# Turned queries in the far stretch, the last pair's sum on VectorE, and a higher rate for the last convolution, in a hybrid encoder layer

## The chip, the cores and the metric

The kernel runs on one core of one Trainium2 chip. The metric is device time in microseconds (us), the median of several executions; lower is better. The engines are TensorE (PE; its weight loads are shown as PEld), VectorE (DVE), ScalarE (ACT), GpSimd (POOL) and SyncE (SP), which issues most of the DMA transfers.

## The reference

One layer on x of 2048 tokens by 1024 channels (cut; everything is float32):

```python
y = rmsnorm(h, norm_mix_g) @ w_in                 # q, k, v (8 heads of 64), conv inputs a, g (512 each)
att = dilated_sliding_attention(q, k, v)          # three patterns, see below
conv = conformer_conv(a, g, ...)                  # a*sigmoid(g), 31 taps per channel, layernorm, silu
h = h + concat([att, conv]) @ w_out
h = h + cross_attention(rmsnorm(h), rmsnorm(mem)) # 4 heads of 256, 256 memory rows
h = h + relu(rmsnorm(h) @ w_up)**2 @ w_down
out = rmsnorm(h)

def dilated_sliding_attention(q, k, v):
    for window, d in ((128, 1), (512, 4), (2048, 16)):
        o, lse = banded_attention(to_strided(q, d), to_strided(k, d), to_strided(v, d), window // (2 * d))
        ...
    w = softmax(stack(lses), axis=0)
    return sum(w[..., None] * stack(outs), axis=0)
```

Pattern d takes every d-th token as a sequence of its own, and each query sees the keys within 64 places of it there. Here pattern 0 is d = 1, pattern 1 is d = 4, and the far pattern is d = 16. The three results of a query are added with weights that come from their log-denominators.

## The kernel before, in words

**Number format.** Every matmul operand is kept as a high and a low part (fp32r), and each product is three matmuls (`mm3`, L197 to L200): high by high, high by low, low by high. A weight tile is loaded raw, its high part is cast on ScalarE (L189), its low part is a subtraction (L190) on VectorE, or on GpSimd for the glu weights.

**Stages.** The first stages normalise x, and compute q, k, the gated convolution inputs u (`glu`) and v, in token groups of 512 (p = 0 to 3). Results go to DRAM scratch (`qscr`, `qfar`, `kscr`, `vtok`, `uscr`) and are read again in the order that each pattern needs. After them:

- *The value stage* (L737 to L747): matmuls of the second half of v. Beside them the convolution of token group 0 for channel tiles 2 and 3 (`conv0`, pinned behind VectorE's last value operation): a multiply-add on VectorE for each of 31 taps (L215), 4 to a step, and the result goes to `cscr`. `weave(steps, (conv0, 1.2))` (L746) takes 1.2 steps of it for each step of the value pipeline, and `drain(conv0)` what is left.
- *The far stretch* (L1082 to L1110): attention of token group 0 (`first = att(0, p2_)`) with the far pattern of all tokens. For each head: four far units (`att_far`), two units of pattern 1, two of pattern 0 (`order` is (1, 0), L941). A unit is: scores of query blocks into PSUM (L979; L845 and L846 for the far pattern), mask and minimum on VectorE (L762), exponential on ScalarE (L763), turns on TensorE (L769), casts (L772, L773), products with the values (L777 to L779). The units are staged so that the scores of one come ahead of the turns of another. `rest`, the remaining glu tiles and the first two output weights, fills TensorE between: 32 steps go ahead, then 0.8 steps for each of `first` (L1107, L1109). A step of `rest` is one `mm3`. `ln0` is the layernorm of group 0's convolution; it reloads `cscr` as tiles `lc` (added at L238 to L240).
- *The post stages*, p = 0 to 3: output projection with residual (`resid_linear`), cross-attention, MLP and final norm. Beside them run the attention of group p + 1, without far pattern, and its convolution. The last steps of `first` are woven with the first of post(0), and the rest of `first` is drained there: the handover.

**Queries.** `load_keys` loads a head's queries (`qh`, high twice; `ql`, low) from `qscr`. In the far stretch both heads of a pair are loaded at the pair's beginning (L1015), the heads in two slots of `qlow`, and pattern 1 takes `slice(blk, 512, 4)` of them as weights (L974): a read with a step of four floats. In the other attention stages `turned` (L806 to L811) lays them out by residue with two GpSimd copies per head, so that pattern 1 reads contiguous queries too.

**The sum of the patterns.** `combine` (L871 to L932) is one generator per pair of heads. It loads patterns 1 and 2 of the pair from DRAM (`ld` from `oscr`), computes the weights (L890 to L912; minima, exponential and reciprocal on VectorE and ScalarE, the other small ones on `W`, which is GpSimd), multiplies and adds the three results (L916, L918, on `W`), turns the sum on TensorE (L926), and splits it into a high part (ScalarE, L928) and a low part (VectorE, L929). Both go to DRAM (`cath`, `catl`). `load_cat` and `load_pair` load them again as operands of the output projection. In post(0) the last of these loads (pair j = 1 of half 1, that is k = 2 and 3) is issued late, ahead of the last two k of the first three output tiles (L1180).

**Order.** The scheduler fixes each engine's order when the program is built; engines then run their queues strictly in order, and a waiting instruction holds all behind it. SyncE's queue issues loads and stores in one order as well. `weave` and `pinned` (issue behind the last recorded instruction of the named engines) steer that order.

Of the kernel before, what the change touches and what calls it, by code (L numbers as in the profile page):

```python
# [21 lines left out]
P = 128  # L22
S = 2048
D = 1024
H = 8
# [22 lines left out]
def hybrid_layer(ctx, tc, A, out):  # L48
# [688 lines left out]
    with ExitStack() as st:  # L737
        lbv = pool("lin_v", stack=st)
        cu = pool("conv0b", stack=st)
        conv0 = pinned(conv_units(cu, 0, (2, 3), False), "dve")  # L740
        for _ in range(4):
            next(steps)
        weave(islice(steps, 8), (conv0, 1))
        for _ in range(4):
            next(steps)
        weave(steps, (conv0, 1.2))  # L746
        drain(conv0)  # L747
    early.close()

# [40 lines left out]
        dma(f(k), f(kscr[:, :, h].rearrange("x d r i -> (x d) r i")[:, :, 32 * p:32 * p + 64]))  # L790
        return k

    def load_keys(h, p, slot=0):

        k = None
        if p:
            k = keys_of(h, p)
        qh = kq.tile([P, 512], F32R, tag="qh", name=f"qh{p}{h}", bufs=2)
        ql = qlow[slot]
        cols = slice(512 * p, 512 * p + 512)  # L800
        for x in range(2):
            dma(f(qh[64 * x:64 * x + 64]), f(qscr[0, :, h, cols]))
        dma(f(ql[0:64]), f(qscr[1, :, h, cols]))
        return k, (qh, ql)
# [21 lines left out]
    def att_far(p2_, h, k, vt, q):  # L826
# [37 lines left out]
        for rq in range(4):  # L864
# [3 lines left out]
            if rq == 2 and h < H - 1:  # L868
                q[0] = far_q(h + 1, 0)

    def combine(p, pr, o0):  # L871

        if p:
            yield
        ld = aq.tile([P, 2, 4, 2, ROW], F32, tag="ld", name=f"ld{p}{pr}")
        for i in range(2):
            dma(ld[:, i].rearrange("p j h e -> p j (h e)"),
                oscr[pr][i][512 * p:512 * (p + 1)].rearrange("(j p) e -> p j e", p=P))
        yield
        yield  # L880
        if p == 0:
            for _ in range(2 if pr < 3 else 1):
                yield
        sm_ = top.tile([P, 5, 8], F32, tag="csm", name=f"csm{p}{pr}")
        e3 = top.tile([P, 3, 4, 2], F32, tag="ce", name=f"ce{p}{pr}")
        mm_ = sm_[:, 0].rearrange("p (j h) -> p j h", h=2)
        W = POOL
        with ExitStack() as st:
            after(st, "dve")
            DVE.tensor_tensor(mm_, ld[:, 0, :, :, HD + 1], ld[:, 1, :, :, HD + 1], op=ALU.min)  # L890
            DVE.tensor_tensor(mm_, mm_, o0[:, :, :, HD + 1], op=ALU.min)
        W.tensor_tensor(e3[:, 0], mm_, o0[:, :, :, HD + 1], op=ALU.subtract)
        for i in range(2):
            W.tensor_tensor(e3[:, 1 + i], mm_, ld[:, i, :, :, HD + 1], op=ALU.subtract)
        yield
        with ExitStack() as st:
            after(st, "act")
            ACT.activation(e3, e3, AF.Exp)
        d3 = sm_[:, 1:4].rearrange("p q (j h) -> p q j h", h=2)
        W.tensor_tensor(d3[:, 0], e3[:, 0], o0[:, :, :, HD], op=ALU.mult)  # L900
        for i in range(2):
            W.tensor_tensor(d3[:, 1 + i], e3[:, 1 + i], ld[:, i, :, :, HD], op=ALU.mult)
        dn = sm_[:, 4]
        W.tensor_tensor(dn, sm_[:, 1], sm_[:, 2], op=ALU.add)
        W.tensor_tensor(dn, dn, sm_[:, 3], op=ALU.add)
        yield
        with ExitStack() as st:
            after(st, "dve")
            DVE.reciprocal(dn, dn)
        d2 = dn.rearrange("p (j h) -> p j h", h=2)  # L910
        for i in range(3):
            W.tensor_tensor(e3[:, i], e3[:, i], d2, op=ALU.mult)  # L912
        at = aq.tile([P, 4, 2, HD], F32, tag="cat", name=f"cat{p}{pr}")
        for i in range(3):
            src = ld[:, i - 1, :, :, 0:HD] if i else o0[:, :, :, 0:HD]
            W.tensor_tensor(src if i else at, src, e3[:, i].unsqueeze(3).to_broadcast([P, 4, 2, HD]), op=ALU.mult)  # L916
            if i:
                W.tensor_tensor(at, at, src, op=ALU.add)  # L918
        yield
        yield  # L920
        ct = [aq.tile([P, 512], F32R, tag=f"ct{x}", name=f"ct{x}{p}{pr}") for x in "hl"]
        with ExitStack() as st:
            after(st, "pe", "act", "dve")
            pt = ps("T", f"catT{p}{pr}")
            for j in range(4):
                PE.transpose(pt[:, j * P:(j + 1) * P], at[:, j].rearrange("p h d -> p (h d)"), ident)  # L926
            vs = vinv[:, pr:pr + 1]
            ACT.activation(ct[0], pt, AF.Copy, scale=vs)  # L928
            DVE.scalar_tensor_tensor(ct[1], pt, vs, f(ct[0]), op0=ALU.mult, op1=ALU.subtract)  # L929
        for t, d in zip(ct, (cath, catl)):  # L930
            dma(f(d[pr][:, 512 * p:512 * (p + 1)]), f(t))
        yield  # L932

    def att_units(p, far, then):
# [25 lines left out]
        def unit(pr, hh, pat, g, k, q_, opt, o0):  # L960
# [6 lines left out]
            for z in range(2):  # L967
                blk = 2 * g + z
                if pat == 0:
                    qs = slice(P * blk, P * blk + P)  # L970
                    kv = k[:, :, 8 * blk + 12:8 * blk + 28].rearrange("p r (c i) -> p c r i", c=2)
                    m = 0 if 4 * p + blk == 0 else (2 if 4 * p + blk == 15 else 1)
                else:
                    qs = slice(P * blk, P * blk + P) if not far else slice(blk, 512, 4)  # L974
                    kv = k[:, blk:16:4, 0:64].rearrange("p r (c i) -> p c r i", c=2)
                    m = 3 if p == 0 else (5 if p == NG - 1 else 4)
                o = sp_[:, 256 * z:256 * z + 256]
                for x in range(2):
                    last["pe"] = PE.matmul(o, q_[x][:, qs], kv, start=x == 0, stop=x == 1)  # L979
                probs.append((pat, m, o, sm[:, 2 * z:2 * z + 2].rearrange("p c q -> p (c q)"),  # L980
                              os_[:, blk, hh, HD + 1:HD + 2]))
# [21 lines left out]
            if g and hh:  # L1003
                if pat == order[1]:
                    then(pr, o0)
                if pr < H // 2 - 1:
                    if not far:
                        load_v(pr + 1, (pat,))
                    elif not pat:
                        load_v(pr + 1, (2, 1, 0))  # L1010

        load_v(0, (2, 1, 0) if far else (0, 1))
        nxt = None if far else load_keys(0, p)
        for pr in range(H // 2):
            K = [load_keys(2 * pr + hh, p, hh) for hh in range(2)] if far else None  # L1015
            o0 = aq.tile([P, 4, 2, ROW], F32, tag="o0", name=f"o0_{p}{pr}", bufs=2)
            for hh in range(2):
                h = 2 * pr + hh
                if far:
                    k, q_ = keys, K[hh][1]  # L1020
                    if h < H - 1:
                        keys = far_keys(far, h + 1)
                    yield from att_far(far, h, k, vt, q3)
                    qs = (q_, q_)
                else:
                    k, q_ = nxt
                    qs = (q_, turned(h, p, q_))
                for pat in order:
                    opt = []
                    yield from [unit(pr, hh, pat, g, k, qs[pat], opt, o0) for g in range(2)]  # L1030
                    if not far and pat == 0 and h < H - 1:
                        nxt = load_keys(h + 1, p)

    def att(p, far=None):

# [46 lines left out]
    with ExitStack() as st:  # L1082
# [2 lines left out]
        qlow3 = low_parts(p2_, 1024, 2, "ql3")  # L1085
        p2_.tile([P, 176], F32, name="farpad")
        rest = pinned(pipeline(*(u for c in range(4) for u in glu(c, (2, 3), True)), ahead(0), ahead(1)), "pe")
        for _ in range(32):
            next(rest)

        c01 = []
# [12 lines left out]

        ln0 = pinned(conv_ln(0, ln_alloc), "pe")
        first = pinned(att(0, p2_), "pe")
        weave(islice(first, 50), (ln0, 0.33), (rest, 0.8))  # L1107
        drain(ln0)
        weave(islice(first, 74), (rest, 0.8))  # L1109
        drain(rest)  # L1110
    lin.close()

# [36 lines left out]
        rstd_col(r[:, 0:n], pc[:, 0:n], n, top)  # L1149
        return r  # L1150

    cats = {}

    def load_cat(p, half):

        d = cats.setdefault(p, {})
# [3 lines left out]
                for e in range(2):  # L1160
                    d[q, 4 * (1 - half) + 2 * j + e] = t[:, e]
        for j in range(2):
            if j == 0 or half == 0 or p:
                load_pair(p, half, j)

    def load_pair(p, half, j):
        for q, src in (("h", cath), ("l", catl)):
            for e in range(2):
                k = 4 * (1 - half) + 2 * j + e
                dma(f(cats[p][q, k]), f(src[k][:, 512 * p:512 * (p + 1)]))  # L1170

    def resid_linear(load, rhs, korder, resid, hs, ssum, key, y, name, late=None):


        for ms in ((0, 1, 2), (3,), (4,), (5,), (6,), (7,)):
            wt = [load(m) for m in ms]
            pts = {}
            for i, ks in enumerate((korder[0:4], korder[4:6], korder[6:8]) if len(ms) > 1 else (korder,)):
                if late and len(ms) > 1 and i == 2:
                    late()  # L1180
                for m, (wh, wl) in zip(ms, wt):
                    if m not in pts:
                        pts[m] = ps("mm", f"{name}{m}")
                    for k in ks:
                        mm3(pts[m], wh[:, k, :], wl[:, k, :], rhs["h", k], rhs["l", k], k == korder[0], k == korder[-1])
                    if late and ks[-1] != korder[-1]:
                        yield
                    if ks[-1] == korder[-1]:
                        h = hs[m]
# [7 lines left out]
    def post(p):  # L1197
# [9 lines left out]
        def from_x(m):  # L1207
# [5 lines left out]
        ssum = ssum_tile(f"o{p}")  # L1213
        yield from resid_linear(lambda m: wout[m] if p == 0 and m in wout else wpost(wcols(w_out, m * P), f"o{p}{m}"),
                                cats[p], [4, 5, 6, 7, 0, 1, 2, 3], from_x, hs, ssum, "x", y, f"o{p}_",
                                (lambda: load_pair(0, 1, 1)) if p == 0 else None)
        rs = rstd_from(ssum)
        DVE.tensor_scalar(rs[:, 4:8], rs[:, 0:4], -1.0, None, op0=ALU.mult)

# [192 lines left out]
```

## Time and profile before

| | us |
|---|---|
| median of 3 runs | 2933.51 |
| lowest, highest | 2924.72, 2937.39 |
| profiled execution | 2929.9 |
| its span in the trace | 2928.1 |

The span is the time from the first to the last instruction of the profiled execution; 1.8 us of that execution lie around it. The mean granted TensorE clock is 0.989 of full speed. In the profile, rows of the order in time give start, duration, engine, line, operation, tiles (out<-in), shapes and, in brackets, how long the engine had been idle and what ended that. Rows by stretch give length, then busy time and number of instructions of PE, PEld, DVE, ACT and POOL, then the granted clock, the share of the DMA engines' time in use and GB/s. Busy time of a pipelined matmul overlaps that of the next: the distance of two starts says what one costs.

### The profile page before, as it was taken

The page shows a single profiled execution, that of the slowest core. Times are in us where ns is not written, and L with a number is a line of the kernel's source. Part 1 is how long each engine was busy: PE and PEld are TensorE (multiplying, and loading weights), DVE is VectorE, ACT ScalarE, POOL GpSimd, SP SyncE. Part 2 cuts the span into 40 slices and gives each one's busy share as a digit, 9 for nine tenths or more (in the row PEclk, how much of TensorE's full clock was granted, in tenths as well). Part 3 has the DMA queues.
Part 4 walks back from the last instruction along what each step waited for, and adds up shares of the span by engine and source line. Part 5 has one row for each costly group of instructions (what it writes and reads, how often), then busy time and mean ns, then how long its engine had stood idle before and what let it go on. Part 6 is the DMA issues. An engine that isn't in the chain of part 4 may idle for free.

```text
span 2928.1 us, 42935 instructions
## 1 busy us (share of the span) xinstructions
PE 2845.6 (97%) x16396; PEld 2426.2 (83%) x16396; DVE 1845.9 (63%) x3295; ACT 1186.9 (41%) x2002; POOL 462.9 (16%) x518
## 2 busy tenths in 40 slices
PE   8999999989799999999999999999999999999999
PEld 7878789878698888888888888888888888888887
DVE  5636544555568877566697865577877555544445
ACT  5632211566435333444443344344433443432233
POOL 1335421122101220210020122000210110000000
PEclk9999999999899999999999999999999999999999
DMA  8978854799724444455344445534444355333332
GB/s 263 304 161 205 194 146 135 172 239 230 206 93 133 129 134 136 138 167 172 97 128 129 136 130 177 181 101 131 121 132 132 113 153 173 94 93 94 96 99 73
DMA packets 620806, 434.89 MB, mean 149 GB/s; under 512 B 191333, under 2 KB 549785, under 8 KB 620600
## 3 DMA queue, kind: packets, MB, share of 16 engines
q1 hardware_dynamic: 582168, 414.05, 50.3%
q10 hardware_dynamic: 38432, 18.09, 2.6%
q8 instruction: 129, 2.11, 0.3%
q14 instruction: 77, 0.63, 0.1%
HBM read 340.42 MB, written 91.64 MB: 148 GB/s over the span
## 4 chain that ended last, share of the span: by engine, by line
PE 75%; DMA 4%; ACT 2%; DVE 2%; SPq 2%; issue 1%; POOL 1%; ACTq 0%; POOLq 0%; DVEq 0%
PE dn L198 8%; PE dn L199 8%; PE dn L200 8%; PE up L198 8%; PE up L200 8%; PE up L199 7%; PE xs L198 2%; PE xs L199 2%; PE xs L200 2%; PE o L198 2%; PE o L199 2%; SPq L57 2%; PE o L200 2%; PE pt L769 2%; PE s L979 2%; PE x L198 2%
## 5 line engine op out<-in xcount | busy, mean ns | idle before, releaser
L198 PE MATMUL up<-mh,whi_u 128*128 128x512 f32 x1024 | 402.9, 394 | 1.3 <-DVE rl L1283 1.1
L199 PE MATMUL dn<-hhl,whi_d 128*128 128x512 f32 (+1 forms) x1056 | 402.5, 385 | 0.4 <-DVE hhl L1286 0.4
L200 PE MATMUL dn<-hhh,wlo_d 128*128 128x512 f32 (+1 forms) x1056 | 401.6, 384 | 0.0
L198 PE MATMUL dn<-hhh,whi_d 128*128 128x512 f32 (+1 forms) x1056 | 400.3, 391 | 0.1
L200 PE MATMUL up<-mh,wlo_u 128*128 128x512 f32 x1024 | 399.4, 390 | 0.0
L199 PE MATMUL up<-ml,whi_u 128*128 128x512 f32 x1024 | 398.6, 389 | 0.0
L215 DVE SCALAR_TENSOR_TENSOR cacc<-cu,cw,cacc 128x512 f32<-128x512 f32 x480 | 387.7, 808 | 5.8
L189 ACT CAST whi_u<-raw_u 128x1024 fp32r<-128x1024 f32 x128 | 134.6, 1052 | 428.2 <-PE dn L199 358.5
L1301 DVE TENSOR_TENSOR h<-h,dn 128x512 f32<-128x512 f32 (+1 forms) x264 | 172.5, 668 | 203.3 <-PE dn L200 202.3
L189 ACT CAST whi_d<-raw_d 128x1024 fp32r<-128x1024 f32 x128 | 134.4, 1050 | 355.4 <-PE up L199 318.3
L200 PEld LDWEIGHTS dn<-hhh,wlo_d 128*128 128x128 f32 x1056 | 198.5, 188 | 39.3
L198 PEld LDWEIGHTS dn<-hhh,whi_d 128*128 128x128 f32 x1056 | 197.5, 188 | 39.3 <-DVE h L1301 3.5
L199 PEld LDWEIGHTS dn<-hhl,whi_d 128*128 128x128 f32 x1056 | 198.8, 188 | 36.4 <-DVE hhl L1286 1.0
L200 PEld LDWEIGHTS up<-mh,wlo_u 128*128 128x128 f32 x1024 | 192.2, 188 | 40.8
L198 PEld LDWEIGHTS up<-mh,whi_u 128*128 128x128 f32 x1024 | 192.1, 188 | 39.9 <-DVE rl L1283 1.8
L199 PEld LDWEIGHTS up<-ml,whi_u 128*128 128x128 f32 x1024 | 192.4, 188 | 38.1
L1283 DVE SCALAR_TENSOR_TENSOR rl<-up,ssumx 128x512 f32<-128x512 f32 x128 | 87.9, 690 | 201.3 <-PE up L200 196.5
L763 ACT ACTIVATE sm<-sm,o 128x256 f32<-128x256 f32 (+1 forms) x384 | 158.9, 465 | 115.3 <-DVE o L762 103.2
L190 DVE TENSOR_TENSOR wlo_u<-raw_u,whi_u 128x1024 fp32r<-128x1024 f32 x128 | 163.5, 1277 | 28.0 <-ACT whi_u L189 27.4
L190 DVE TENSOR_TENSOR wlo_d<-raw_d,whi_d 128x1024 fp32r<-128x1024 f32 x128 | 159.0, 1242 | 28.6 <-ACT whi_d L189 28.6
L762 DVE CUSTOM_DVE_ANT_0 sm<-s,mask 128x256 f32<-128x256 f32 (+1 forms) x384 | 127.8, 375 | 54.1 <-PE s L979 34.3
L198 PE MATMUL xs<-whi_a,yh 128*128 128x256 f32 x512 | 146.7, 289 | 1.3 <-DVE o L762 1.3
(390 smaller groups left out, 6498.4 us busy)
## 6 DMA issues: line engine op xcount, KB each, us to landing
raw_u<-in_w_up_dram SPq DMA_DIRECT2D x128, 512.0 KB
raw_d<-in_w_down_dram SPq DMA_DIRECT2D x128, 512.0 KB
raw_o<-in_w_out_dram SPq DMA_DIRECT2D x32, 512.0 KB
raw_a<-ascr SPq DMA_DIRECT2D x32, 512.0 KB
raw_b<-bscr SPq DMA_DIRECT2D x32, 512.0 KB
v<-vtok SPq DMA_DIRECT2D x208, 65.0 KB
k<-kscr SPq DMA_DIRECT2D x24, 512.0 KB
k<-kscr SPq DMA_DIRECT2D x8, 1152.0 KB
```

The lines of the kernel that those rows point to most:

```text
L57: (q or nc.sync).dma_start(o, i)
L189: ACT.copy(hi, raw)
L190: (lo_eng or DVE).tensor_tensor(lo, raw, f(hi), op=ALU.subtract)
L198: PE.matmul(o, lh, rh, start=first, stop=False)
L199: PE.matmul(o, lh, rl, start=False, stop=False)
L200: last["pe"] = PE.matmul(o, ll, rh, start=False, stop=end)
L215: DVE.scalar_tensor_tensor(acc, u[:, t:t + 512], cw[:, c, t:t + 1], acc, op0=ALU.mult, op1=ALU.add)
L762: last["dve"] = DVE.tensor_tensor_reduce(dst, so, mask[:, 256 * m:256 * m + nk], 1.0, 3e38, ALU.add, ALU.min, mn)
L763: last["act"] = ACT.activation(dst, dst, AF.Exp, bias=mn, scale=-1.0)
L769: last["pe"] = PE.transpose(pt[:, j, :], sm[:, j, :], ident)
L1283: last["dve"] = DVE.scalar_tensor_tensor(r, pt, 0.0, rsb, op0=ALU.max, op1=ALU.mult)
L1301: last["dve"] = DVE.tensor_tensor(hs[m][:, sl], hs[m][:, sl], pt, op=ALU.add)
```

## The change

Four things change.

1. The value stage's convolution runs at rate 2.2 instead of 1.2 (L746), and the far stretch takes 38 steps of `rest` ahead instead of 32, then 0.75 per step instead of 0.8.
2. In the far stretch pattern 1 uses turned queries as well. A head's queries are loaded and turned (`both_q`) after pattern 0 of the head before, not at the pair's beginning; `load_keys` has one low slot, the other holds the turned low part. That is two GpSimd copies (L810) per head, 16 in all. The order of the patterns stays (1, 0).
3. For group 0's last pair, `combine` computes on VectorE (`W = DVE`; 16 operations), and writes the high and low parts into the operand tiles of the output projection. Their store and reload (two transfers each) go.
4. `load_pair(0, 1, 1)` loads k = 2 alone, with the others, not late. The flag that makes `resid_linear` yield between parts of the first three tiles is called `steps`.

```diff
-        weave(steps, (conv0, 1.2))
+        weave(steps, (conv0, 2.2))
...
-    def load_keys(h, p, slot=0):
+    def load_keys(h, p):
...
-        ql = qlow[slot]
+        ql = qlow[0]
...
-        W = POOL
+        end = p == 0 and pr == H // 2 - 1
+        W = DVE if end else POOL
...
-        ct = [aq.tile([P, 512], F32R, tag=f"ct{x}", name=f"ct{x}{p}{pr}") for x in "hl"]
+        ct = [cats[0][x, pr] if end else aq.tile([P, 512], F32R, tag=f"ct{x}", name=f"ct{x}{p}{pr}") for x in "hl"]
...
-        for t, d in zip(ct, (cath, catl)):
+        for t, d in () if end else zip(ct, (cath, catl)):
...
-                    qs = slice(P * blk, P * blk + P) if not far else slice(blk, 512, 4)
+                    qs = slice(P * blk, P * blk + P)
...
+        def both_q(h):
+            k, q = load_keys(h, p)
+            return k, q, turned(h, p, q)
+
         load_v(0, (2, 1, 0) if far else (0, 1))
-        nxt = None if far else load_keys(0, p)
+        nxt = both_q(0) if far else load_keys(0, p)
         for pr in range(H // 2):
-            K = [load_keys(2 * pr + hh, p, hh) for hh in range(2)] if far else None
...
-                    if not far and pat == 0 and h < H - 1:
-                        nxt = load_keys(h + 1, p)
+                    if pat == 0 and h < H - 1:
+                        nxt = both_q(h + 1) if far else load_keys(h + 1, p)
...
-        for _ in range(32):
+        for _ in range(38):
...
-        weave(islice(first, 50), (ln0, 0.33), (rest, 0.8))
+        weave(islice(first, 50), (ln0, 0.33), (rest, 0.75))
         drain(ln0)
-        weave(islice(first, 74), (rest, 0.8))
+        weave(islice(first, 74), (rest, 0.75))
...
-            if j == 0 or half == 0 or p:
-                load_pair(p, half, j)
+            load_pair(p, half, j)
...
-            for e in range(2):
+            for e in range(1 if p == 0 and half and j else 2):
...
-    def resid_linear(load, rhs, korder, resid, hs, ssum, key, y, name, late=None):
+    def resid_linear(load, rhs, korder, resid, hs, ssum, key, y, name, steps=False):
...
-                if late and len(ms) > 1 and i == 2:
-                    late()
```

More of the change, by code (lines that the diff above doesn't have):

```diff
@@ L869, in att_far @@
                 q[0] = far_q(h + 1, 0)
+    cats = {}
     def combine(p, pr, o0):
@@ L1018, in att_units @@
                 h = 2 * pr + hh
+                k, *qs = nxt
                 if far:
-                    k, q_ = keys, K[hh][1]
+                    k = keys
                     if h < H - 1:
@@ L1023, in att_units @@
                     yield from att_far(far, h, k, vt, q3)
-                    qs = (q_, q_)
                 else:
-                    k, q_ = nxt
-                    qs = (q_, turned(h, p, q_))
+                    qs.append(turned(h, p, qs[0]))
                 for pat in order:
@@ L1150, in rstd_from @@
         return r
-    cats = {}
     def load_cat(p, half):
@@ L1177, in resid_linear @@
             pts = {}
-            for i, ks in enumerate((korder[0:4], korder[4:6], korder[6:8]) if len(ms) > 1 else (korder,)):
-                if late and len(ms) > 1 and i == 2:
-                    late()
+            for ks in (korder[0:4], korder[4:6], korder[6:8]) if len(ms) > 1 else (korder,):
                 for m, (wh, wl) in zip(ms, wt):
@@ L1185, in resid_linear @@
                         mm3(pts[m], wh[:, k, :], wl[:, k, :], rhs["h", k], rhs["l", k], k == korder[0], k == korder[-1])
-                    if late and ks[-1] != korder[-1]:
+                    if steps and ks[-1] != korder[-1]:
                         yield
@@ L1215, in post @@
                                 cats[p], [4, 5, 6, 7, 0, 1, 2, 3], from_x, hs, ssum, "x", y, f"o{p}_",
-                                (lambda: load_pair(0, 1, 1)) if p == 0 else None)
+                                p == 0)
         rs = rstd_from(ssum)
```

## The prediction

> **What bounds the kernel now.** I read the page first, then the busy time by stretches, then the order in time at the places where TensorE stands idle. From the page:
>
> ```profile
> span 2928.1 us, 42935 instructions
> PE 2845.6 (97%) x16396; PEld 2426.2 (83%) x16396; DVE 1845.9 (63%) x3295; ACT 1186.9 (41%) x2002; POOL 462.9 (16%) x518
> PE 75%; DMA 4%; ACT 2%; DVE 2%; SPq 2%; issue 1%; POOL 1%; ACTq 0%; POOLq 0%; DVEq 0%
> ```
>
> TensorE is busy for 97% of the span and makes 75% of the chain that ended last. So a change pays in two ways only: less TensorE time, or less of its idle 3%. Everything that the diff touches lies before 800 us; behind it TensorE goes on in the same order, so what is won or lost by then should reach the end undiminished. The stretches (length; busy us of PE, PEld, DVE, ACT, POOL; granted clock; DMA share; GB/s):
>
> ```profile
> 560.00:745.00 185.00, 170.33 (x1518) 147.02 (x1517) 109.09 (x446) 128.60 (x284) 37.47 (x57) 0.97 0.92 229
> 745.00:760.00 15.00, 14.23 (x88) 11.70 (x87) 7.07 (x24) 5.38 (x10) 2.18 (x2) 0.89 1.03 224
> 760.00:775.00 15.00, 9.10 (x66) 7.20 (x64) 6.44 (x15) 4.78 (x13) 3.39 (x12) 0.90 0.68 174
> 775.00:790.00 15.00, 5.15 (x34) 3.65 (x35) 4.19 (x9) 2.18 (x4) 7.24 (x7) 0.50 0.62 174
> ```
>
> The first row is nearly the whole far stretch: TensorE is busy for 170.3 of 185 us, but the DMA share is 0.92. The last two are the handover to the first output projection: TensorE works 14.25 of 30 us, and in the last at half clock. TensorE there, in order of time:
>
> ```profile
> 775.84 0.21 PE L777 MATMUL opt<-v,ph 128*128 128x65 f16 x1 [6.75 <-DMA v<-vtok]
> ...
> 782.29 1.11 PE L926 MATMUL catT<-ident,cat 128*128 128x128 f32 x4 [4.19 <-POOL cat L918]
> ...
> 789.10 1.65 PE L198 MATMUL o<-cath,whi_o 128*128 128x512 f32 x3 [0.88 <-DMA cath<-cath]
> ...
> 791.40 0.63 PE L199 MATMUL o<-catl,whi_o 128*128 128x512 f32 x1
> 791.83 0.63 PE L200 MATMUL o<-cath,wlo_o 128*128 128x512 f32 x1
> ...
> 792.62 0.39 PE L200 MATMUL o<-cath,wlo_o 128*128 128x512 f32 x1
> 792.85 0.40 PE L198 MATMUL o<-cath,whi_o 128*128 128x512 f32 x1
> ```
>
> It waits 6.75 us for a value load, 4.19 for the last pair's sum on GpSimd, then for the sum's way through DRAM. A 128x512 matmul starts 0.43 us after the one before (791.40 to 791.83) until the clock is given back, then 0.23 (792.62 to 792.85).
>
> **Part A: conv0 at 2.2, six more steps ahead.** Before the far stretch TensorE and VectorE show this:
>
> ```profile
> 539.23 0.28 PE L846 MATMUL s<-k,ql 128*128 128x256 f32 x1
> 543.16 0.38 PE L845 MATMUL s<-k,qh 128*128 128x256 f32 x1 [3.65 <-DVE o L762]
> ...
> 543.99 0.63 PE L198 MATMUL lin<-xh,whi_g 128*128 128x512 f32 x1
> ```
> ```profile
> 517.28 5.47 DVE L215 SCALAR_TENSOR_TENSOR cacc<-cu,cw,cacc 128x512 f32<-128x512 f32 x7
> ```
> ```profile
> 541.91 0.69 DVE L240 TENSOR_TENSOR lsum<-lsum,lc 128x512 f32<-128x512 f32 x1 [3.30 <-DMA lc<-cscr]
> ```
> ```profile
> 522.78 0.32 SPq L57 DMA_DIRECT2D cscr<-cacc  x1
> ...
> 535.44 0.58 SPq L57 DMA_DIRECT2D lc<-cscr  x1
> ```
> ```profile
> 538.27 1.28 ACT L763 ACT_TABLE_LOAD   x1
> ```
> ```profile
> 543.00:548.00 5.00, 4.83 (x22) 4.29 (x23) 1.85 (x12) 2.40 (x7) 0.00 (x0) 0.66 0.77 208
> 769.00:793.00 24.00, 8.24 (x43) 5.99 (x43) 9.28 (x18) 4.66 (x8) 10.63 (x18) 0.57 0.64 174
> ```
>
> Seven convolution instructions are left over when the value projection ends; they run until 522.75, and only then can their result be stored (522.78). Its reload is issued at 535.44, behind far keys and queries in the same queue, and the add that wants it (L240) holds VectorE's in-order queue until 541.91, with the first far scores' exponent minima behind it. TensorE idles 3.65 us, and the matmuls after it have the 0.63 us length of half clock, as above: the granted clock of the 5 us from 543 on is 0.66, so 5 x 0.34 = 1.7 us more are lost. At rate 2.2 the seven go among the value tiles, where 0.78 us each (5.47/7) has to fit into VectorE's free time; the store and the reload then stand ahead of the far keys in the queue and L240 ahead of the scores. Won: 3.65 + 1.7 = 5.35 us. The new order on ScalarE puts a sigmoid with its two table loads behind the first eight exponentials: one load is 1.28 us, and what the stretch's filler doesn't cover of it I estimate at 1.3 us. **A = 4.0 us, from 0** (VectorE holds the value tiles up instead) **to 5.4**. The six steps are 18 matmuls of 0.23 us = 4.1 us, moved and not saved: nothing, since the rate falls from 0.8 to 0.75 with it; if the filler then runs out early, it costs these 4.1 us at most.
>
> **Part B: turned queries.** Weight loads of pattern-1 scores take every fourth query; those of pattern 0 are contiguous:
>
> ```profile
> 579.30 0.31 PEld L979 LDWEIGHTS s<-k,qh 128*128 128x128 f32 x1
> 579.53 0.31 PEld L979 LDWEIGHTS s<-k,ql 128*128 128x128 f32 x1
> 579.75 0.33 PEld L979 LDWEIGHTS s<-k,qh 128*128 128x128 f32 x1
> 579.99 0.33 PEld L979 LDWEIGHTS s<-k,ql 128*128 128x128 f32 x1
> ```
> ```profile
> 562.69 0.19 PEld L979 LDWEIGHTS s<-k,qh 128*128 128x128 f32 x1
> 562.81 0.19 PEld L979 LDWEIGHTS s<-k,ql 128*128 128x128 f32 x1
> ```
>
> They last 0.31 to 0.33 us against 0.19, and follow each other after 0.23 us against 0.12. There are 64 of them (8 heads, 2 units, 2 blocks, 2 parts): 64 x 0.107 = 6.9 us. The Trainium skill, "SBUF — State Buffer", section "Door 1: The DMA port swizzle", says that the step that costs nothing "depends on dtype: 4 fp32", which is this very step; by it this part would give 0 and the sum 12.0 instead of 16.5. The trace disagrees, with 0.31 against 0.19 us, and the measurement decides.
>
> Not all of the 6.9 shows up: the stretch has 14.7 us of idle (185 less 170.3), which sits where TensorE waits for ScalarE and VectorE to finish a unit; scores that are through sooner lengthen some of these waits. **B = 4.5 us, from 0 to 6.9.** The added work is 16 copies on GpSimd, 1.07 us each (row 779.01 below), 17 us beside 37.5 us busy of 185: hidden as long as the queries arrive in time. They are now loaded after pattern 0 of the head before. The shortest lead in the trace, and a load in a crowded stretch:
>
> ```profile
> 724.95 0.19 PEld L979 LDWEIGHTS s<-k,ql 128*128 128x128 f32 x1
> ```
> ```profile
> 739.25 0.31 PEld L979 LDWEIGHTS s<-k,qh 128*128 128x128 f32 x1
> ```
> ```profile
> 750.59 0.43 SPq L57 DMA_DIRECT2D raw_o<-in_w_out_dram  x1
> ```
> ```profile
> 758.24 1.05 ACT L189 CAST whi_o<-raw_o 128x1024 fp32r<-128x1024 f32 x1 [5.54 <-DMA raw_o<-in_w_out_dram]
> ```
>
> The lead is 14.3 us here and 16.5 for head 1 (562.81 to 579.30). Landing took 7.65 us (750.59 to 758.24), two copies 2.1: 9.8 us. The cover holds by 4.5 us. If it failed: a waiting copy stands at the head of GpSimd's queue, with the low parts of the filler's weights and the other pairs' sums behind it.
>
> **Part C: last pair's sum on VectorE, kept on chip.**
>
> ```profile
> 774.44 1.04 POOL L916 TENSOR_TENSOR cat<-o,ce 128x512 f32<-128x512 f32 x1
> ...
> 777.89 1.17 POOL L918 TENSOR_TENSOR cat<-cat,ld 128x512 f32<-128x512 f32 x1
> 779.01 1.07 POOL L810 CAST qt<-qh 128x512 fp32r<-128x512 f32 x1
> ...
> 781.07 1.17 POOL L918 TENSOR_TENSOR cat<-cat,ld 128x512 f32<-128x512 f32 x1
> ```
> ```profile
> 769.16 0.17 DVE L890 TENSOR_TENSOR csm<-ld 128x8 f32<-128x8 f32 x1 [2.10 <-DMA ld<-oscr]
> ...
> 784.16 0.75 DVE L929 SCALAR_TENSOR_TENSOR ctl<-catT,vinv,cth 128x512 fp32r<-128x512 f32 x1 [6.85 <-ACT cth L928]
> ```
>
> The parts arrive at 769.16 and the fourth output tile starts at 792.85: 23.7 us. The five large operations take GpSimd from 774.44 to 782.24, two query copies among them (779.01 to 781.07): 7.8 us. VectorE's same form is 0.69 us (L240): 5 x 0.69 = 3.45, **4.35 saved**. The eleven small ones before (from 769.3 to 774.4, with VectorE's reciprocal between) cost 0.17 each on VectorE, 1.9 with hops to and from ScalarE on top; convolution instructions of 0.78 us may stand between: nothing to 3 saved, I take 0.9. The way through DRAM, from the low part's end at 784.91 to 789.10, goes: **4.2 saved**. Against it stand 1.3 us of the next attention that now come after the tile's last matmuls are ready: a turn of four, 1.11 at half clock as in row 782.29, so 0.56 at full, and 24 value products 0.03 apart (775.84 to 775.87). Together 4.35 + 0.9 + 4.2 - 1.3 = **8.1 us, say 8.0, from 4** (VectorE's queue holds the sum as long as GpSimd did, only the way through DRAM is saved) **to 10**. What is late next is the value load: it let TensorE go at 775.84, 6.7 us after the parts came, and isn't moved ahead.
>
> **Sum:** 4.0 + 4.5 + 8.0 = 16.5 us. Against the profiled execution (2929.9, that is the span 2928.1 and 1.8 around it) 2913.4; that execution lies 3.6 under the median of the three runs, so against the median of 2933.5 it is **2917**. About 0.5%, 14.7 us, is what a measurement of this kernel can tell from no change.
>
> **The rivals.**
> - *Absorbed.* The far stretch is bound by its transfers (share 0.92 over 185 us, 1.03 in the next 15); scores that are done sooner wait for keys, values or weights, and the sum on VectorE finds only the way through DRAM. A part of A, nothing of B, most of C: 8 to 12 us, 2923.5. For it: the DMA share; against it: TensorE's 92% of the same stretch.
> - *Clock too.* The half-clock spell ends at 792.6 because TensorE idles on and off from 769.1. If the new gaps are short enough, it shrinks: two turns of four at 1.11 would take half, 1.1 less, and seven matmuls at 0.43 would take 0.23, 1.4 less, with some 0.5 on the value products 3 us; with all three parts at their upper ends 5.4 + 6.9 + 10 + 3 = 25 us, 2908. The Trainium skill, "TensorE: Matmul & The Clock Gate", section "What's actually happening", gives the rule that one idle window of about 3.4 us halves the clock. The trace agrees so far: the gap of 3.65 us is followed by half clock, and 769 to 793 as a whole has 0.57.
> - *Slower: GpSimd's queue held by the turned copies.* At each of seven heads the copies wait for the query load. Decisive is landing plus 2.1 us against the lead: from a landing of 12.2 us on (14.3 less 2.1) the pattern-1 scores wait, and TensorE's order is fixed, so filler and far units behind them wait as well. At 15 us it is 3 us a head, 7 x 3 = 21; with the weights' low parts late behind the same copies up to 5 us a head, 35. Less A and C (12) that is 9 to 23 us slower: 2943 at the nearer end, 2957 at the other. For it: loads issued into a DMA share of 0.92 and a queue that is itself held; against it: the landing of 7.65 in the same crowd.
>
> **How the numbers follow.** Forecast 0.42 (11 to 21 us won; 0.27 over the bound, 0.15 under it), clock too 0.11, absorbed 0.23, slower 0.24 (0.10 over the bound, 0.14 under it). Faster by over 0.5%: 0.27 + 0.11 = 0.38. Within: 0.15 + 0.23 + 0.14 = 0.52. Slower: 0.10. The range, 2905 to 2943, leaves out the upper half of the slower case and a little of the fastest; the forecast's own range is 2912 to 2923.
>
> **What the changed profile would show.** A: no gap of over 2 us between 535 and 550, L240 ahead of the far scores' minima, no convolution run of seven on VectorE. B: L979's loads in the far stretch at 0.19 us throughout; TensorE's pattern-1 scores not released by GpSimd. C: L916 and L918 of the last sum on VectorE at about 0.69 us, no store and reload of the last quarter, parts' arrival to fourth output tile about 16 us instead of 23.7. Wrong would be: pattern-1 scores or filler matmuls waiting for L810 or for a low part on GpSimd (slower), the far stretch as long as before with its idle time up by what B saved (absorbed), or a difference that arises behind 800 us, which nothing here accounts for.

## The result: slower by 0.35%, and the profile after

The changed kernel takes 2941.73 us (median of 10 runs, 2934.87 to 2948.81), the kernel before 2930.74 (10 runs beside them): a ratio of 1.0035, 95% interval 1.002 to 1.005, some 10 us slower. The forecast was 16.5 us faster. The profiled executions differ by more, 2942.5 against 2928.1 us of span, so single traces are used below for places and mechanisms, and the ratios of the repeated runs for sizes (0.1% is 2.9 us). The page of the changed kernel:

```profile
span 2942.5 us, 42954 instructions
PE 2851.0 (97%) x16396; PEld 2427.4 (82%) x16396; DVE 1849.2 (63%) x3311; ACT 1187.0 (40%) x2002; POOL 472.0 (16%) x518
PE 79%; DMA 3%; ACT 2%; DVE 2%; issue 1%; SPq 1%; POOL 0%; ACTq 0%; POOLq 0%; DVEq 0%
```

The chain has lost no TensorE share; the page alone doesn't say where the time went. The far stretch does. To compare the two, I take it between the same two events: the second head's first far score and the first matmul of the output projection. The kernel before (columns as above: length, busy PE, PEld, DVE, ACT, POOL, granted clock, DMA share, GB/s):

```profile
564.80:744.80 180.00, 165.33 (x1472) 142.97 (x1469) 104.10 (x434) 125.01 (x277) 37.47 (x57) 0.97 0.93 234
```

The changed kernel:

```profile
564.40:766.00 201.60, 166.89 (x1450) 140.41 (x1449) 106.39 (x436) 124.20 (x278) 50.52 (x70) 0.92 0.87 210
```

Both reach the first event at the same time, 564.8 and 564.4 us, and the second 21 us apart. TensorE's idle time in the stretch (length less busy) rises from 14.7 to 34.7 us, and its clock falls from 0.97 to 0.92, some 11 us more at half clock's loss (201.6 x 0.08 = 16 against 180 x 0.03 = 5). TensorE's work there fell all the same: busy less the clock's loss is 160 us before and 151 after. The bytes are equal: 180.0 x 234 and 201.6 x 210 are both 42 MB.

Behind it, 8 us come back in the handover (part C). VectorE and TensorE there, in the changed kernel:

```profile
790.17 0.17 DVE L893 TENSOR_TENSOR csm<-ld 128x8 f32<-128x8 f32 x1 [8.95 <-DMA ld<-oscr]
...
793.48 0.69 DVE L919 TENSOR_TENSOR cat<-o,ce 128x512 f32<-128x512 f32 x1
794.09 1.29 DVE L919 TENSOR_TENSOR ld<-ld,ce 128x512 f32<-128x512 f32 x2
...
797.27 0.69 DVE L921 TENSOR_TENSOR cat<-cat,ld 128x512 f32<-128x512 f32 x1
```
```profile
790.69 0.39 PE L982 MATMUL s<-k,ql 128*128 128x256 f32 x1 [3.72 <-DMA ql<-qscr]
796.32 0.69 PE L769 MATMUL pt<-ident,sm 128*128 128x128 f32 x2 [4.26 <-ACT sm L763]
799.09 1.05 PE L929 MATMUL catT<-ident,cat 128*128 128x128 f32 x4
800.92 1.65 PE L198 MATMUL o<-cath,whi_o 128*128 128x512 f32 x3 [0.67 <-ACT cath L931]
...
805.61 0.48 PE L198 MATMUL o<-cath,whi_o 128*128 128x512 f32 x1
```

From the parts' arrival (790.17) to the fourth output tile (805.61) it is 15.4 us, against 23.7 before: 8.3 gained, forecast 8.0. And part A's gap is gone: the add of the reloaded convolution stands at 519, and the far scores' minima begin when the scores are there.

```profile
519.15 0.69 DVE L240 TENSOR_TENSOR lsum<-lsum,lc 128x512 f32<-128x512 f32 x1 [2.33 <-DMA lc<-cscr]
...
542.30 0.29 DVE L762 CUSTOM_DVE_ANT_0 sm<-s,mask 128x128 f32<-128x128 f32 x1 [3.80 <-PE s L846]
```

So two gains came as worked out, and the stretch between them lost more than both. What stands out in it is an idle spell of 5.64 us at the boundary of the second and third pair of heads, TensorE first, then VectorE:

```profile
679.83 1.11 PE L769 MATMUL pt<-ident,sm 128*128 128x128 f32 x4 [5.64 <-ACT sm L763]
```
```profile
678.67 0.17 DVE L893 TENSOR_TENSOR csm<-ld 128x8 f32<-128x8 f32 x1 [6.45 <-DMA ld<-oscr]
```

TensorE waits for exponentials. The profile names VectorE's sum (L894) as what ended ScalarE's idle time ahead of them, but the minima that they need were done by 672.2. ScalarE, the minima's last operation, and the chain that ended last there (start, length, what):

```profile
670.94 0.36 ACT L857 COPY o<-opt 128x260 f32<-128x260 f32 x1
678.85 0.37 ACTq L57 DMA_DIRECT2D oscr<-o  x1
679.27 0.91 ACT L763 ACTIVATE sm<-sm,o 128x256 f32<-128x256 f32 x2 [7.97 <-DVE csm L894]
```
```profile
671.79 0.42 DVE L762 CUSTOM_DVE_ANT_0 sm<-s,mask 128x256 f32<-128x256 f32 x1
```
```profile
674.91 3.86 DMA v<-vtok
678.78 0.02 issue
678.80 0.02 ACTq L57
678.85 0.37 ACTq L57
```

From 671.3 on ScalarE's queue is held by a store that it issues itself (`oscr<-o`). The store waits for the landing of a value load that SyncE issued at 674.91; nothing that it writes comes from that load, but in the trace the two report their landing on the same semaphore. The exponentials start 0.05 us after the store is issued. Beside this VectorE's queue is held by the first operation of the finished pair's sum (L893; L890 before), whose parts haven't landed, and the minima of the next scores stand behind it. Both holds stand at the first pair's boundary too: VectorE until 614.71, after 3.83 us, and ScalarE until its store at 615.35, after 5.9. In the far stretch of the kernel before, VectorE waits ahead of this operation for 1.1 us at most, and these stores hold ScalarE for 3.2 us at most.

### The profile page after: what moved, and what is told of

Read it like the earlier page. It is cut to its first block, busy times and chain, and to the rows that moved or that the text cites. A ratio compares the mean times of both kernels' runs of the same rounds, so it can differ in the third digit from the quotient of the medians.

```text
span 2942.5 us, 42954 instructions
## 1 busy us (share of the span) xinstructions
PE 2851.0 (97%) x16396; PEld 2427.4 (82%) x16396; DVE 1849.2 (63%) x3311; ACT 1187.0 (40%) x2002; POOL 472.0 (16%) x518
## 4 chain that ended last, share of the span: by engine, by line
PE 79%; DMA 3%; ACT 2%; DVE 2%; issue 1%; SPq 1%; POOL 0%; ACTq 0%; POOLq 0%; DVEq 0%
PE dn L198 8%; PE dn L199 8%; PE dn L200 8%; PE up L198 8%; PE up L200 8%; PE up L199 8%; PE xs L198 2%; PE xs L199 2%; PE xs L200 2%; PE o L198 2%; PE o L199 2%; PE o L200 2%; PE x L198 2%; PE x L199 2%; PE x L200 2%; PE pt L769 2%
```

## The experiments

Each ratio is to the kernel before, run beside it on the same chip, with its 95% interval. The difference of two such ratios, from which variants are compared below, is uncertain by 0.13 to 0.2%, 4 to 6 us; a difference of two such differences by some 7 us. "A's rate" is conv0 at 2.2, "the steps" are 38 ahead at 0.75.

### First set: which part

**A alone** (`a_alone`: the two diffs of part A on the kernel before).

> The kernel before with part A alone (conv0 rate 2.2, 38 steps ahead, rate 0.75). Theory 1 (the loss of the changed kernel comes from the far stretch's queries, part B): no gap before the far scores, about 4 us faster than before, 0 to 5.4. Rival 2 (the loss comes from A: the moved filler shifts the weight loads and stores of the far stretch): 10 to 20 us slower, with the loss between 600 and 740 us.

Measured 1.0032 (1.002 to 1.0045), 9 us slower.

**B alone** (`b_alone`: `both_q`, `load_keys` and the contiguous `qs` of the change on the kernel before).

> The kernel before with part B alone (far queries loaded after pattern 0 of the head before, and turned). Theory 1: slower by 15 to 22 us, the far stretch longer by about 20 with VectorE and ScalarE held by DMA waits at the pairs' beginnings. Rival 2 (A is the cause): 0 to 7 us faster, by the turned weight loads.

Measured 1.0044 (1.0027 to 1.006), 13 us slower.

**C alone** (`c_alone`: `end`, `W`, `ct` into `cats`, and the loads of `load_pair` on the kernel before).

> The kernel before with part C alone (last pair's sum on VectorE, parts kept on chip). Both theories: about 8 us faster, all of it between the last far scores and the fourth output tile. If C depends on A or B, less than 4.

Measured 0.9992 (0.9982 to 1.0002): not to be told from no change, though in its trace the way from the parts to the fourth tile is 17.8 us instead of 23.7.

**A and C** (`no_b`: the changed kernel with part B undone).

> The changed kernel with part B undone (A and C kept). Theory 1: 12 us faster than before (8 to 15), that is about 22 faster than the changed kernel. Rival 2: slower than before by 2 to 10 us. If the parts only hurt together, somewhere between.

Measured 1.0010 (1.000 to 1.0019). Theory 1 and its rival are both wrong as far as they name one part: A costs as well as B, and the parts don't add up (0.32 + 0.44 - 0.08 is 0.68%, measured 0.35%).

### Second set: A and B taken apart

**A's rate alone**:

```diff
-        weave(steps, (conv0, 1.2))
+        weave(steps, (conv0, 2.2))
```

> The kernel before with conv0 at rate 2.2 and nothing else. The prediction's step A: the gap before the far scores goes, 4 us faster (0 to 5.4). Theory 3 (the far stretch's waits swallow or return what is won ahead of it): 0 to 2 us faster.

Measured 0.9985 (0.9976 to 0.9994): 4.4 us faster (1.8 to 7.0); forecast 4.0. It shows up whole, which theory 3 did not expect. The single traces don't show that: the second head's first far score comes 5.1 us earlier (559.6), but the stretch behind it is 186.2 us long instead of 180.0.

**The steps alone** (38 ahead, 0.75, rate 1.2 kept).

> The kernel before with only the filler moved: 38 steps ahead, rate 0.75. The prediction: no change. Theory 3 (this filler covered TensorE's waits in the far stretch; without it the waits stand open, and half-clock spells follow them): 8 to 13 us slower, with about 7 us more idle time between the second far head and the output projection. Rival 4 (A's loss comes from the convolution's rate): within 3 us of before.

Measured 1.0020 (1.0011 to 1.0029): 6 us slower. Rival 4 is out.

**The changed kernel with the steps taken back**:

```diff
-        for _ in range(38):
+        for _ in range(32):
...
-        weave(islice(first, 50), (ln0, 0.33), (rest, 0.75))
+        weave(islice(first, 50), (ln0, 0.33), (rest, 0.8))
...
-        weave(islice(first, 74), (rest, 0.75))
+        weave(islice(first, 74), (rest, 0.8))
```

> The changed kernel with 32 steps ahead and rate 0.8 as before (conv0 at 2.2, B and C kept). Theory 3: 8 to 13 us faster than the changed kernel, that is within 3 us of the kernel before. Rival 4: as slow as the changed kernel.

Measured 0.9973 (0.9963 to 0.9983): faster than the kernel before by 8 us, and than the changed one by 0.62%, 18 us. Those six steps turn the sign of the whole change.

**B's late loads without turning** (`both_q` returns the loaded queries twice, the strided `qs` stays; on the kernel before).

> The kernel before with B's late loads alone: queries loaded after pattern 0 of the head before, but not turned, strided weight loads kept. If B's loss comes from when the queries are loaded (SyncE's queue held, transfers behind it late): as slow as B alone, 10 to 20 us slower than before. If it comes from the copies, or from scores that are faster than what follows them (cover gone, then half clock): within 4 us of before.

Measured 1.0009 (1.000 to 1.0019). The later loads alone cost little; most of B's loss when it stands alone comes only with the copies and the faster scores, which this run doesn't tell apart.

### Third set: cover in the stretch, or what stands ahead

**Less filler**, nothing moved (A's rate, B, C, 32 steps; six products of the glu tiles left out):

```diff
+            if not (skip and k == 3):
+                mm3(pt, wh[:, k, :], wl[:, k, :], XH_[k, n], XL_[k, n], k == 0, k == KC - 1)
...
+                for _ in linear_steps(pt, wh, wl, n, fine and c > 0 and n == 2):
```

> The changed kernel with 32 steps ahead and rate 0.8, and six mm3 steps of the glu filler left out inside the far stretch (six glu tiles lack one of eight products): as little filler in the stretch as in the changed kernel, but nothing moved ahead of it. Theory 3 (the filler in the stretch is the cover): no gain for 4.1 us less TensorE work, or slower, by up to 10 us against the same kernel with all its filler (0.9973 of before). Rival 5 (the loss comes from what stands ahead: the far stretch, and its transfers, start 4 to 8 us later): as fast as that kernel or up to 4 us faster.

Measured 0.9962 (0.995 to 0.9975): 3 us faster than with all the filler, though the intervals overlap. So theory 3 doesn't explain the 18 us: with the stretch as thin as in the changed kernel there is no loss.

**Filler done twice**, 38 ahead (the changed kernel at 0.8, with six steps repeated in the stretch):

```diff
+        if twice:
+            mm3(pt, wh[:, 0, :], wl[:, 0, :], XH_[0, n], XL_[0, n], True, True)
+            yield
```

> The changed kernel with 38 steps ahead as it has, but rate 0.8 and six filler steps in the stretch done twice: the stretch has as much filler as before, and starts later as in the changed kernel. Theory 3: about 4 us (the added work) slower than with 32 steps ahead, that is 0.998 to 1.000 of before. Rival 5: as slow as the changed kernel, 1.003 to 1.005 of before.

Measured 1.0018 (1.0009 to 1.0027): 13 us slower than with 32 ahead, of which 4.1 are the added work. So about 9 of the 18 us come with what stands ahead of the stretch, whatever cover is left in it; the rest is between the two theories.

**26 steps ahead, 0.85**:

> The changed kernel with 26 steps ahead and rate 0.85: six steps moved into the stretch instead of out of it. Theory 3: as fast as with 32 steps (0.9973 of before) or up to 8 us faster. If the stretch is bound by its TensorE work there: about 4 us slower than with 32.

Measured 0.9981 (0.9972 to 0.999), the same as with 32 within the intervals.

**A's rate and C, without B, 32 ahead**:

> Conv0 at 2.2 and part C, without B, 32 steps ahead: what B is worth beside them. If B's gain in TensorE time is absorbed: as fast as the same with B (0.9973 of before, within 0.1%). The prediction's step B: 4.5 us slower than with B (0.9988). If B costs by its later loads also here: faster, 0.994 to 0.996.

Measured 0.9960 (0.9947 to 0.9974), the fastest of all, 12 us under the kernel before. Against it B costs 0.13%, 4 us, with intervals that overlap, where 4.5 us of gain were forecast; with the steps it costs 0.25%, 7 us (1.0035 against 1.0010). Against A's rate alone, C gives 0.25%, 7 us.

The stretch between the same two events shows where B's gain goes. A's rate and C without B:

```profile
560.60:742.40 181.80, 166.31 (x1476) 143.23 (x1472) 105.02 (x438) 125.12 (x277) 37.47 (x57) 0.97 0.94 232
```

The same with B:

```profile
555.70:744.20 188.50, 162.61 (x1472) 138.63 (x1468) 104.17 (x438) 125.75 (x279) 51.72 (x70) 0.95 0.92 224
```

Busy less the clock's loss falls from 160.9 to 153.2 us, about the forecast 6.9 (the clock's two digits leave 1 us open). The idle time rises from 15.5 to 25.9, and the kernel with B, 5 us ahead at the start, is 2 behind at the end.

### Fourth set: what holds the stretch

**Later sums** (on the changed kernel):

```diff
-            for _ in range(2 if pr < 3 else 1):
+            for _ in range(5 if pr < 3 else 1):
```

> The changed kernel with the sums of pairs 0 to 2 started three steps later, so that VectorE reaches their first operation about 3 us later. Theory 6 (in the changed kernel VectorE's queue is held by that first operation until its parts land, 3.8 and 6.4 us in the trace, and the far scores behind it wait): 4 to 9 us faster than the changed kernel, 1.0005 to 1.002 of before, and no VectorE wait for these parts. If the hold only takes the place of another wait for the same transfers: within 2 us of the changed kernel.

Measured 1.0009 (1.000 to 1.0018): 0.26%, 7.6 us, faster than the changed kernel. VectorE no longer waits for the parts in the far stretch, and TensorE's idle time between the same two events falls from 34.7 to 26.6, the clock staying where it was:

```profile
565.30:755.80 190.50, 163.92 (x1452) 140.49 (x1450) 104.97 (x435) 123.22 (x278) 50.74 (x70) 0.92 0.92 222
```

ScalarE's hold at the second boundary falls with it, from 7.6 to 3.6 us, so the gain can't be put down to VectorE alone. No run moved ScalarE's stores; what they cost is not known.

**No table loads, 38 ahead**, and the same with 32 ahead (the sigmoid of the far stretch's glu tiles is left out, an exponential stands in its place):

```diff
-                    ACT.activation(sig[n], pt, AF.Sigmoid)
+                    ACT.activation(sig[n], pt, AF.Exp if fine else AF.Sigmoid, scale=0.01 if fine else 1.0)
```

> The changed kernel (38 steps ahead) with the far stretch's glu gate computed with an exponential of a hundredth in place of the sigmoid, so that no activation table is loaded there (12 loads of 1.28 us fewer). Theory 7 (the six steps shift the table loads into the way of the far scores' exponentials): 10 to 15 us faster than the changed kernel, as fast as the same kernel with 32 steps (within 4 us). If the loads have no part in it: up to 4 us faster, and the two step counts stay 15 us or more apart.

> The same with 32 steps ahead and rate 0.8. Theory 7: 0 to 5 us faster than with the sigmoid (0.9973 of before), so 0.9955 to 0.9975. If the loads have no part: the same range, but the kernel with 38 steps stays 15 us or more slower.

Measured 1.0002 (0.9993 to 1.0011) with 38 and 0.9963 (0.995 to 0.9975) with 32. Without the loads the first gains 0.33%, the second 0.10%, and they stay 0.39% apart. By these numbers the loads' place could be a third of the steps' cost; the difference between the two gains, 0.23%, is no more than its uncertainty, and the single traces have it the other way (the stretch is 2.7 us shorter without the loads at 38 steps, 7.5 at 32). That the steps cost some 11 us without these loads is clear. With 32 steps and no loads, B's turned queries kept, the stretch goes through in 181.0 us:

```profile
560.50:741.50 181.00, 160.46 (x1475) 137.68 (x1471) 104.99 (x436) 113.12 (x269) 51.76 (x70) 0.96 0.96 233
```

One place of such loads, ScalarE and TensorE in the changed kernel:

```profile
563.38 1.28 ACT L507 ACT_TABLE_LOAD   x1
564.67 0.60 ACT L507 ACTIVATE sig<-lin 128x512 f32<-128x512 f32 x1
565.17 0.58 ACT L772 CAST ph<-pt 128x512 f16<-128x512 f32 x1
565.77 1.28 ACT L763 ACT_TABLE_LOAD   x1
567.06 0.91 ACT L763 ACTIVATE sm<-sm,o 128x256 f32<-128x256 f32 x2
```
```profile
567.62 0.84 PE L769 MATMUL pt<-ident,sm 128*128 128x128 f32 x4 [1.58 <-ACT sm L763]
```

The two loads and the sigmoid put 3.2 us ahead of the exponentials that the turn waits for, and TensorE stands 1.58 us.

**48 steps ahead, 0.67**:

> The changed kernel with 48 steps ahead (three whole glu passes of 16, as 32 is two) and rate 0.67. Theory 7 (the phase of the glu passes against the far units): between 32 and 38 steps, 0.998 to 1.002 of before. If each step ahead costs more than its work (cover gone, transfers later): slower than with 38 steps, 1.007 to 1.012 of before.

Measured 1.0026 (1.0017 to 1.0036), as with 38. The loss neither grows with each step nor goes when whole passes are moved; this kernel also has four table loads fewer than the others (19 instead of 23).

### Fifth set

**Steps taken back and later sums**:

> The changed kernel with 32 steps ahead, rate 0.8, and the sums of pairs 0 to 2 started three steps later. Theory 6 (B's 6 us of TensorE time is lost to VectorE's queue held by the sums' first operation): faster than with 32 steps alone (0.9973 of before) by 3 to 7 us, 0.995 to 0.9963, as fast as A's rate and C without B (0.996) or faster. If the hold only stands in for the transfers behind it: 0.9965 to 0.998.

Measured 0.9964 (0.9951 to 0.9978): 0.09% under the kernel without the later sums, with intervals that overlap, and equal to the kernel without B. The stretch:

```profile
558.50:746.60 188.10, 163.84 (x1475) 138.24 (x1471) 103.21 (x436) 123.74 (x278) 51.65 (x70) 0.96 0.95 224
```

It is as long as with the earlier sums (188.1 against 188.5), with 24.3 us idle against 25.9: with 32 ahead, other waits take the hold's place. Theory 6 fits the changed kernel, where ScalarE's hold fell as well, and not this one.

**Most of the first output weight's load left out** (on the changed kernel):

```diff
-        dma(raw, wcols(w_out, m * P))
+        if m:
+            dma(raw, wcols(w_out, m * P))
+        else:
+            dma(raw[:, 0], w_out[0:P, 0:P])
+            POOL.memset(raw[:, 1:8], 0.0)
```

> The changed kernel (38 steps ahead) with seven eighths of the first output weight's load left out (those rows are zeroed on GpSimd instead), so that the pair boundary at about 655 us moves 448 KB less. Theory 8 (with 38 steps this load stands ahead of the far keys and the parts, and makes them late): 5 to 10 us faster than the changed kernel, 1.000 to 1.002 of before. If that load has no part in it: within 2 us of the changed kernel.

Measured 1.0028 (1.0019 to 1.0037): 2 us faster than the changed kernel, against 5 to 10 forecast by theory 8. That load is not the cause of the 18 us; a part of up to 5 us isn't excluded.

## Why the prediction was wrong, step by step

- **In all.** Each taken on the one before: A's rate won 4.4 us, C 7.3, B lost 3.8, and the six steps lost 18.2. That is 10.3 us slower, where 16.5 faster was forecast.
- **A, the rate: right.** 4.4 us measured alone, 4.0 forecast; the gap and its half-clock spell went as read.
- **A, the six steps: the step that failed.** The prediction put them at nothing ("moved and not saved"), with 4.1 us as the worst. Measured: 6 us alone, 14 beside the rate (1.0032 against 0.9985), 15 beside rate and C (1.0010 against 0.9960), 18 with everything. The six products were counted as TensorE time alone; that they set the place of all else in the stretch was left out. In the traces of these four pairs the second head's first far score comes 0.7 to 8.8 us later with the steps, and the stretch behind it takes 2 to 13 us longer although it holds 4 us less of TensorE's work. Two things in the stretch are candidates, neither clear of noise as a part of the steps' cost: the first operations of the pairs' sums (moving them later gives 0.26% with the steps and 0.09% without, 5 us of difference, uncertain by 7) and the places of the glu's table loads (0.33% against 0.10%, 7 us, uncertain by 7). A third, ScalarE's stores that wait for value loads, no run tested. Nor is it simply that work ahead is paid in full: taking as much work out of the stretch gained about 3 us, ten more steps ahead cost nothing more, and six fewer ahead won nothing. The mechanism stays open.
- **B: the weight loads right, the value wrong.** The loads take 0.19 us and TensorE saves about 7 us, as forecast; with 32 steps all of it and 3 to 4 us more return as idle time, and 4 us go to the lower clock. The prediction's range for B ended at 0; measured are losses of 13 us alone, 7 with A and C, and 4 (not clear of 0) with the steps taken back. The rival "absorbed" named transfers as the bound, with the DMA share of 0.92 as its sign; I gave it 0.23 because TensorE was busy for 92% of the same time. For it: no kernel here got its 42 MB through the stretch at more than 234 GB/s, or in less than 180 us. Against it as the whole account: the changed kernel ran at 210 GB/s and a share of 0.87, and with 32 steps and without the table loads B went through in 181.0 us instead of 188.5. No run took bytes out of the whole stretch, so what paces it is argued and not shown.
- **C: right beside the other parts.** 8.3 us in the trace, 7 between two ratios (0.9985 and 0.9960), 8.0 forecast. Alone it is 2 us and can't be told from nothing; its trace has 5.9 us won in the handover and a far stretch 2.7 us longer. Why is not known.
- **The slower rival** came near in size and failed in its place. It had the turned copies held on GpSimd and pattern-1 scores behind them. The copies do wait long, but no TensorE wait of over 0.4 us in the far stretch ends with L810. What waits is VectorE, for parts that are loaded behind the queries, keys and values in the same queue, and ScalarE, with stores behind value loads.
- **Clock too** went the other way: the half-clock share of the far stretch rose, and gave away some 11 us in the profiled execution.

The version to keep has A's rate and C, 32 steps ahead and no turned queries: 0.9960 of the kernel before. With turned queries and later sums it is 0.9964, the same within the intervals.

## What to carry to other kernels

Before work is saved in a stretch or moved ahead of it, ask what paces that stretch: where other engines and transfers hold TensorE up, saved work can come back as idle time. Filler that moves by a few steps shifts everything tied to it, here table loads, the first operations of sums that wait for a transfer at the head of an in-order queue, and stores that hold the queue of the engine that issues them. When an engine's wait has a named releaser, compare when its inputs were done: here the hold was a store in the engine's own queue. Test the smallest part of a change by itself: here six steps of filler cost more than all the rest won.

## What the runs showed of the hardware

- Half clock follows short gaps as well. The 1.58 us gap of the changed kernel that ends at 567.62, with 0.27 us just before it, is followed by this:

```profile
569.00:573.00 4.00, 4.00 (x20) 3.40 (x19) 2.54 (x11) 3.05 (x9) 0.00 (x0) 0.57 0.36 80
```

TensorE is busy for all of these 4 us, at a clock of 0.57. A stall of 1.58 us so was followed by a further loss of 1.7 us (4.0 x 0.43). The rule that the prediction drew on from the Trainium skill, "TensorE: Matmul & The Clock Gate", section "What's actually happening", speaks of one idle window of about 3.4 us; here a spell of less than half that was enough. The kernel before has it too, after a gap of 1.58 us, so its trace agreed with the rule less than the prediction says:

```profile
649.02 0.59 PE L769 MATMUL pt<-ident,sm 128*128 128x128 f32 x2 [1.58 <-ACT sm L763]
```
```profile
649.20:652.50 3.30, 3.30 (x21) 2.95 (x21) 0.69 (x1) 1.93 (x5) 0.00 (x0) 0.50 1.03 238
```

Not every such gap is followed by half clock. In the 20 traces of this case the granted clock changes on a grid of 3.41 us, each trace with a start of its own. Of the stretches of this grid at full clock between 100 and 850 us, half clock followed all 105 with 2.0 us or more of TensorE idle time in them, added up (the ends of matmuls are modelled), 68 of 206 with 1.0 to 2.0 us, and 1 of 3798 with less.
- A store can hold the engine that issues it: ScalarE stood for 7.6 us ahead of `oscr<-o` (671.3 to 678.85), whose data were done, until a value load of another queue had landed.
- Turned queries load as fast as contiguous ones, and a step of four floats doesn't: weights of the changed kernel's pattern-1 scores start 0.11 to 0.12 us apart, against 0.23 with the step.

```profile
609.43 0.19 PEld L982 LDWEIGHTS s<-k,ql 128*128 128x128 f32 x1
609.54 0.19 PEld L982 LDWEIGHTS s<-k,qt 128*128 128x128 f32 x1
609.66 0.19 PEld L982 LDWEIGHTS s<-k,ql 128*128 128x128 f32 x1
```
